# A macaron encoder block on one core: the opening pinned in written order with TensorE spreading the norm's gain row, and the mLSTM's score and state-read products issued in turn on two row halves

## The chip, the cores and the metric

One core of a Trainium2 chip runs the whole block in one launch. The metric is device microseconds from start to end of the program. The kernel before was run three times: 926.23, 925.30 and 924.71 us, median 925.3. One further execution was taken with the hardware profiler; all views and rows are of that one.

## The reference

Input x is 512 tokens of 1024 features, float32. The block adds three branches in turn:

```python
h = swiglu(rmsnorm(x, norm_ffn1_pre), w_ffn1_in, w_ffn1_out)
x = x + 0.5 * rmsnorm(h, norm_ffn1_post)
h = mixer(rmsnorm(x, norm_mix_pre), ...)
x = x + rmsnorm(h, norm_mix_post)
h = swiglu(rmsnorm(x, norm_ffn2_pre), w_ffn2_in, w_ffn2_out)
x = x + 0.5 * rmsnorm(h, norm_ffn2_post)
```

The feed-forward width is 2816. The mixer joins a gated convolution of three taps over 512 channels with an mLSTM of 4 heads (64 features of q and k, 128 of v) that runs forward and backward over the tokens. The mLSTM is computed in four chunks of 128 tokens. In each head and direction: scores `q kT` inside a chunk, weighted by a decay matrix and multiplied by v; a state `kT v` per chunk, carried from chunk to chunk; and the read of the state carried in, `q C`, added to the chunk's own part and divided by a denominator.

## The kernel before

**Layout and stages.** Tokens lie in four blocks of 128 (`tb`). A feed-forward net has its 2816 columns in 22 pairs of gate and up columns (`j`). Each pair of 128 columns is a product over 1024 features, on two row halves of 256 tokens (`th`). Weights stream from memory through SP's queue (`w_load`, L128 to L139), and every weight and activation is split into a high part (a cast on ACT, L273) and a low part (the difference, on VectorE or, for the first weights, on POOL: L274 and `ON_POOL`), so that a product is three: high by high, high by low, low by high. `w_get` takes a ready weight from a list and splits further ones ahead of need.

The first two pairs (`PLAIN`, four weights) are plain products, L421: for each of the four weights 24 products on tokens 0 to 255, then 24 each on tokens 256 to 511. From the third pair on, the products are those of a seven-product scheme (L400), for which `combine_x` (L325) forms sums of the normed x on VectorE.

**The opening.** SP issues x0 and x1 in halves, then the gain row of the first norm copied to all 128 partitions (L249, two halves of 256 KB), two weights, x2, x3, two weights, and then small vectors (L640 to L646), the gain `g_post1` and the gate weights `rawg`. TensorE meanwhile runs 24 products on zeros (L269). `pre_norm` (L348) squares a token block on ACT (L294), makes the scale on VectorE and POOL (L282, L284, L287), and multiplies x, scale and gain on VectorE (L353). `flip_q` (L314) turns the normed block feature-first: four transposes per half on TensorE into one bank (L318), a high cast on ACT, a low difference on VectorE, and a full copy on ACT (L323). Blocks 0 and 1 are turned ahead of the first product, blocks 2 and 3 between plain products, by hooks `(i, third)`: in the hook's place, ahead of a third of the i-th group of products.

**The mixer.** Columns of the convolution are products at L391 (`mm_cols`), interleaved by hand with the heads. `weigh_q` (L893) multiplies q by its decay: a tile per pair of heads holds, on rows 0 to 63 and 64 to 127, the two heads, and on its column halves the two directions (L902). `states` (L932) makes the states, two heads on two column halves of the array. `head_a(h)` makes the scores of one head, four chunks into one bank (L949), the decay's exponent (L954, then L956 on VectorE reading that bank), and their product (L966). `head_b(h)` makes P times V (L980, 8 products) and adds the state reads (L987, 6 products), then divides (L997 to L1008). `head_c` turns the head (L1021). `conv` has its taps at L838, L840 and L842.

Scores and reads contract over 64 features, so each uses half the rows of the array: `qk[es, ...]` with `es` the rows of the head.

**What sets the order.** The code is written out by hand, and the framework's scheduler orders the instructions on each engine by its own timeline; PSUM has eight banks in one pool, SBUF pools of a few buffers, and a new tile waits until the readers of the tile that last held its buffer are done.

## Time and profile before

| | |
|---|---|
| timed runs | 926.23, 925.30, 924.71 us; median 925.3 |
| profiled execution | 924.99 us, of it 923.3 in the span of its instructions |
| first product of the first pair (L421) | starts at 13.15 us |
| first product of the seven-product scheme (L400) | starts at 39.76 us |
| first scores (L949) to last reads (L987) | 442.5 to about 511.6 us |
| TensorE's waits for other engines, as the waits view lists them | 10.3 us in seven groups, 4.0 of them L318 for L353 |

A row of the timeline or the chain gives the start, the duration, the engine and the line, the tiles written and read, how many instructions are joined, and in brackets how long the engine was idle before and for whom it waited. A row of the groups gives, after the bar, busy time and mean duration in ns, and then idle time ahead of it. A row of the windows gives the busy time of TensorE (with how many instructions), of its weight loads, VectorE, ACT and POOL, and then the granted clock as a share of full speed, the DMA share and rate. Matmuls are pipelined: durations overlap, and the pace is read from the length of a chain piece divided by its count.

### The profile page before, as it was taken

How to read it: one execution, taken by the hardware profiler on the slowest of the kernel's cores; microseconds unless marked ns; L12 is line 12 of the kernel's file. 1: busy time of each engine (PE TensorE's matmuls, PEld its weight loads, DVE VectorE, ACT ScalarE, POOL GpSimd, SP SyncE). 2: the span in 40 equal slices, each digit the busy share in tenths (PEclk: the TensorE clock that was granted, in tenths of full speed). 3: DMA queues.
4: the chain of work that ended last, by engine and by line, in shares of the span. 5: the costliest groups of instructions: out<-in, count | busy, mean ns of one | idle time of the engine just before them, and what ended most of it. 6: DMA issues, size and time to landing. Idle time of an engine off the chain costs nothing.

```text
span 923.3 us, 15016 instructions
## 1 busy us (share of the span) xinstructions
PE 906.5 (98%) x6015; PEld 822.4 (89%) x6015; DVE 713.2 (77%) x1192; ACT 446.4 (48%) x753; POOL 42.3 (5%) x64
## 2 busy tenths in 40 slices
PE   7999999999999999999999999999999999999997
PEld 7999999999877888987888888999999999977885
DVE  5988988888988358496777736889888888999434
ACT  6645555555456226452424425645545544565311
POOL 3000000000012001000011000000000000000000
PEclk9999999999999999999999999999999999999999
DMA  8433434343344514231422501314343333343502
GB/s 246 146 92 92 138 105 125 92 117 95 100 136 139 180 46 115 61 100 46 117 90 69 160 23 30 104 51 137 92 129 101 109 104 97 106 149 100 172 4 88
DMA packets 126542, 96.99 MB, mean 105 GB/s; under 512 B 4212, under 2 KB 114824, under 8 KB 126472
## 3 DMA queue, kind: packets, MB, share of 16 engines
q1 hardware_dynamic: 126472, 96.03, 35.2%
q8 instruction: 47, 0.77, 0.3%
q14 instruction: 23, 0.19, 0.1%
HBM read 93.92 MB, written 2.10 MB: 104 GB/s over the span
## 4 chain that ended last, share of the span: by engine, by line
PE 89%; DVE 6%; ACT 1%; DMA 1%; issue 1%; SPq 0%; POOL 0%; DVEq 0%; POOLq 0%; ACTq 0%
PE ps L400 42%; PE ps L550 13%; PE ps L391 12%; PE ps L525 8%; PE ps L1063 5%; PE ps L421 4%; PE ps L913 2%; DVE big L274 2%; DVE wlo L274 2%; DVE big L492 1%; DMA raw<-in_w_ffn_in_dram 1%; PE ps L980 1%; PE ps L987 1%; PE ps L318 1%; ACT whi L273 0%
## 5 line engine op out<-in xcount | busy, mean ns | idle before, releaser
L274 DVE TENSOR_TENSOR wlo<-raw,whi 128x1024 fp32r<-128x1024 f32 x209 | 247.3, 1192 | 63.7 <-ACT whi L273 47.1
L273 ACT CAST whi<-raw 128x1024 fp32r<-128x1024 f32 x211 | 211.9, 1029 | 153.0 <-DVE raw L150 46.8
L400 PE MATMUL ps<-big,whi 128*128 128x256 f32 x1920 | 264.9, 280 | 0.0
L400 PEld LDWEIGHTS ps<-big,whi 128*128 128x128 f32 x1920 | 243.4, 188 | 0.9 <-ACT whi L273 0.2
L400 PE MATMUL ps<-big,wlo 128*128 128x256 f32 x960 | 150.9, 280 | 0.0
L400 PEld LDWEIGHTS ps<-big,wlo 128*128 128x128 f32 x960 | 129.2, 188 | 0.0
L550 PE MATMUL ps<-whi,big 128*128 128x512 f32 x384 | 122.3, 396 | 0.2 <-ACT whi L273 0.2
L550 PEld LDWEIGHTS ps<-whi,big 128*128 128x128 f32 x384 | 72.0, 188 | 17.7 <-ACT whi L273 0.7
L391 PE MATMUL ps<-big,whi 128*128 128x512 f32 (+1 forms) x384 | 79.8, 358 | 0.0
L525 PE MATMUL ps<-whi,big 128*128 128x512 f32 x240 | 76.1, 395 | 2.8 <-ACT big L273 2.6
L550 PE MATMUL ps<-wlo,big 128*128 128x512 f32 x192 | 75.6, 395 | 0.0
L391 PEld LDWEIGHTS ps<-big,whi 128*128 128x128 f32 x384 | 63.5, 188 | 10.8 <-issue 0.2
L400 PE MATMUL ps<-big,ws 128*128 128x256 f32 x480 | 65.3, 280 | 0.0
L400 PEld LDWEIGHTS ps<-big,ws 128*128 128x128 f32 x480 | 60.3, 188 | 0.0
L525 PEld LDWEIGHTS ps<-whi,big 128*128 128x128 f32 x240 | 44.7, 188 | 13.8 <-ACT big L273 3.5
L462 ACT COPY t<-ps 128x256 f32<-128x256 f32 x40 | 14.9, 372 | 71.4 <-PE ps L400 71.3
L273 ACT CAST big<-big 128x512 fp32r<-128x512 f32 (+2 forms) x68 | 36.1, 583 | 22.7 <-DVE big L492 11.2
L525 PE MATMUL ps<-wlo,big 128*128 128x512 f32 x120 | 44.8, 393 | 0.0
L550 PEld LDWEIGHTS ps<-wlo,big 128*128 128x128 f32 x192 | 36.1, 188 | 8.5
L391 PE MATMUL ps<-big,wlo 128*128 128x512 f32 (+1 forms) x192 | 41.1, 356 | 0.0
L274 DVE TENSOR_TENSOR big<-big,big 128x512 fp32r<-128x512 f32 (+2 forms) x68 | 40.7, 635 | 0.1
L391 PEld LDWEIGHTS ps<-big,wlo 128*128 128x128 f32 x192 | 32.1, 188 | 5.5
(207 smaller groups left out, 1149.6 us busy)
## 6 DMA issues: line engine op xcount, KB each, us to landing
raw<-in_w_ffn_in_dram SPq DMA_DIRECT2D x88, 512.0 KB, 4.8
raw<-in_w_ffn_out_dram SPq DMA_DIRECT2D x44, 512.0 KB, 4.3
raw<-in_w_mix_in_dram SPq DMA_DIRECT2D x24, 512.0 KB, 3.7
raw<-in_w_mix_out_dram SPq DMA_DIRECT2D x8, 512.0 KB, 3.4
raw<-in_w_ffn_out_dram SPq DMA_DIRECT2D x10, 256.0 KB, 4.2
out_dram<-x SPq DMA_DIRECT2D x8, 256.0 KB, 2.9
x<-in_x_dram SPq DMA_DIRECT2D x4, 256.0 KB, 4.5
x<-in_x_dram SPq DMA_DIRECT2D x2, 512.0 KB
```

The lines of the kernel that those rows point to most:

```text
L273: nc.scalar.copy(out=hi, in_=src)
L274: eng.tensor_tensor(out=lo, in0=src, in1=f32(hi), op=ALU.subtract)
L318: nc.tensor.transpose(out=pt[:, blk(k)], in_=xs[:, blk(4 * b + k)], identity=ident)
L391: nc.tensor.matmul(o, ww[:, k, :], xk(xT, xx, k, sl), start=n == 0, stop=n == 3 * KD - 1)
L400: nc.tensor.matmul(o, ww[:, k, :], x[xx][:, k, :], start=first and n == 0, stop=n == 11, skip_group_check=True)
L421: nc.tensor.matmul(o, ww[:, k, :], xq_hl(xq, (k // 4, th))[xx][:, k % 4, :], start=n == 0, stop=n == 3 * KD - 1)
L462: nc.scalar.copy(a_[:, h1], x[:, h0])
L492: nc.vector.tensor_tensor(out=o, in0=a_, in1=b_, op=op)
L525: nc.tensor.matmul(acc[tb + t][half], left[n][x][:, blk(t)], right[n][y], start=first and x == y == 0, stop=last_ and x == 1, skip_group_c ...
L550: nc.tensor.matmul(acc[tb][half], hT[hh][:, blk(tb)], w[ww][:, blk(half, 512)], start=fresh and hh == ww == 0, stop=k == NF - 1 and hh == ...
L913: nc.tensor.matmul(pv_, xk(xT, xx, k, blk(tb)), ww[:, k % 2, :], start=n == 0, stop=n == 3 * KD - 1)
L1063: nc.tensor.matmul(acc[half], yy[yi][:, k % 4, blk(tb)], wmo[k][wi][:, blk(half, 512)], start=(n == 0 and yi == 0 and wi == 0), stop=(n == ...
```

## The change

Two parts, which touch different stages.

**Opening.** All instructions ahead of the first seven-product are pinned in the order in which the code issues them. The gain row comes as one row of 4 KB, first on SP; TensorE spreads it by two float32 products of a column of ones with it, into two banks, after 12 of now 20 warm products, and VectorE reads the gain from PSUM. Blocks 0 and 1 are turned block by block instead of half by half, into four banks of their own, and their full copies move from ACT to VectorE. All four first weights have their low part on POOL. x2 and x3 are squared in one piece. The small vectors and two gains are issued later on SP, and the weights between x2 and x3.

**Mixer.** The q tile has directions on its row halves and heads on its column halves. Scores of both heads of a pair are issued in turn, chunk by chunk, each to its own bank, at the even head. The states are made per head with the two directions on the column halves. The state reads of both directions of one head are issued in turn on the two row halves.

```diff
-WARM = 24
+WARM = 20
-ON_POOL = (0, 1)
+ON_POOL = (0, 1, 2, 3)
...
+    g_row = gbp.tile([P, D], F32, tag="gb", name="g_row")
+    nc.sync.dma_start(g_row[0:1, :], a["norm_ffn1_pre"])
     x_load(0, 2)
     x_load(1, 2)
-    g_pre = gain("norm_ffn1_pre", 2)
     w_load(2)
     x_load(2)
+    w_load(1)
     x_load(3)
-    w_load(2)
+    w_load(1)
...
+    first = [ps() for _ in range(4)]
+    g_pre = [ps() for _ in range(2)]
+    for n in range(WARM):
+        pin(nc.tensor.matmul(pw[:, 0:256], warm[:, 0:P], warm, start=True, stop=True))
+        if n == 11:
+            for i in range(2):
+                pin(nc.tensor.matmul(g_pre[i], ones, g_row[0:1, blk(i, 512)], start=True, stop=True))
...
+    full = []
+    for tb in range(2):
+        for b in range(2):
+            full.append(flip_q(tb, xs[tb], xT1, (b,), first[2 * tb + b]))
+        if tb == 0:
+            for i in range(WARM2):
+                pin(nc.tensor.transpose(out=pw[:, 0:P], in_=xs[0][:, blk(i % 4)], identity=ident))
+        w_split(1)
+    for fn in full:
+        fn()
...
-                nc.vector.tensor_tensor(out=qt[:, blk(d, 512)], in0=pi, in1=qk[:, pr, 0:512], op=ALU.mult)
+                for e in range(2):
+                    es, ds = slice(e * DK, (e + 1) * DK), slice(d * DK, (d + 1) * DK)
+                    nc.vector.tensor_tensor(out=qt[ds, blk(e, 512)], in0=pi[es], in1=qk[es, pr, 0:512], op=ALU.mult)
...
-        pS = ps()
-        for c in range(NT):
-            nc.tensor.matmul(pS[:, blk(c)], qk[es, 2 + pr, blk(c)], qk[es, pr, blk(c)], start=True, stop=True)
+        if e == 0:
+            both = [ps(), ps()]
+            for c in range(NT):
+                for o in range(2):
+                    os_ = slice(o * DK, (o + 1) * DK)
+                    nc.tensor.matmul(both[o][:, blk(c)], qk[os_, 2 + pr, blk(c)], qk[os_, pr, blk(c)], start=True, stop=True)
+            scores[h], scores[h + 1] = both
+        pS = scores.pop(h)
...
-        for d in range(2):
-            for c in range(NT):
-                if before[d][c] >= 0:
-                    nc.tensor.matmul(
-                        dest[d][c], qt_pair[pr][es, d * 512 + c * P:d * 512 + (c + 1) * P],
-                        Cs[es, 2 * d + pr, before[d][c], :], start=False, stop=True, skip_group_check=True,
-                    )
+        for n in range(NT - 1):
+            for d in range(2):
+                c = [c for c in range(NT) if before[d][c] >= 0][n]
+                ds = slice(d * DK, (d + 1) * DK)
+                nc.tensor.matmul(
+                    dest[d][c], qt_pair[pr][ds, e * 512 + c * P:e * 512 + (c + 1) * P], Cs[ds, h, before[d][c], :],
+                    start=False, stop=True, skip_group_check=True,
+                )
```

In the changed kernel the lines have moved: L269 is L285, the spreading products are L288, L318 is L343, L353 is L383, L421 is L453, L400 is L431, L391 is L422, L949 is L1003, L956 is L1012, L987 is L1043, and L840 is L890. Three places on the engines:

TensorE at the start, from the last warm products to the first products; in the kernel before:

```order
L269 MATMUL ps_115<-warm 128x256
L318 MATMUL ps_167<-ident,t_7_141 128x128 x4
L610 MATMUL ps_115<-ident,t_7_141 128x128 x4
L318 MATMUL ps_181<-ident,t_13_154 128x128 x4
L318 MATMUL ps_189<-ident,t_7_141 128x128 x4
L318 MATMUL ps_199<-ident,t_13_154 128x128 x4
L421 MATMUL ps_247<-big_172,whi_235 128x256 x4
```

and in the changed one, from the twelfth warm product (eight warm products stand behind the two that spread the gain, of which the last is shown; `t_12` is the normed block 0, `t_18` block 1):

```order
L285 MATMUL ps_116<-warm 128x256
L288 MATMUL ps_121<-g_row,ones 128x512
L288 MATMUL ps_122<-g_row,ones 128x512
...
L285 MATMUL ps_116<-warm 128x256
L343 MATMUL ps_117<-ident,t_12_146 128x128 x4
L343 MATMUL ps_118<-ident,t_12_146 128x128 x4
L650 MATMUL ps_116<-ident,t_12_146 128x128 x4
L343 MATMUL ps_119<-ident,t_18_159 128x128 x4
L343 MATMUL ps_120<-ident,t_18_159 128x128 x4
L453 MATMUL ps_235<-big_176,whi_192 128x256 x4
```

Both halves of block 0 are now turned ahead of block 1, and the gain's two products stand inside the warm ones. The second place is TensorE from the scores of head 1 to the reads of head 0, which follow them (`t_663` and, after, `t_661` is head 0's weighted score tile); before:

```order
L949 MATMUL ps_4871<-big_4301 128x128 x4
L954 MATMUL ps_4877<-big_4311 128x512
L954 MATMUL ps_4886<-big_4311 128x512
L980 MATMUL ps_4896<-big_4318,t_663_4730 128x129 x2
L980 MATMUL ps_4897<-big_4318,t_663_4730 128x129 x2
L980 MATMUL ps_4902<-big_4318,t_663_4730 128x129 x2
L980 MATMUL ps_4903<-big_4318,t_663_4730 128x129 x2
L987 MATMUL ps_4896<-big_4573,qt_4629 128x129
L987 MATMUL ps_4897<-big_4573,qt_4629 128x129 x2
L987 MATMUL ps_4902<-big_4573,qt_4629 128x129 x2
L987 MATMUL ps_4903<-big_4573,qt_4629 128x129
```

and after, where the scores of head 1 were made with those of head 0, so that only head 1's exponent and head 0's P times V and reads stand here:

```order
L1010 MATMUL ps_4874<-big_4304 128x512
L1010 MATMUL ps_4883<-big_4304 128x512
L1035 MATMUL ps_4893<-big_4311,t_661_4732 128x129 x2
L1035 MATMUL ps_4894<-big_4311,t_661_4732 128x129 x2
L1035 MATMUL ps_4899<-big_4311,t_661_4732 128x129 x2
L1035 MATMUL ps_4900<-big_4311,t_661_4732 128x129 x2
L1043 MATMUL ps_4893<-big_4566,qt_4622 128x129
L1043 MATMUL ps_4899<-big_4566,qt_4622 128x129
L1043 MATMUL ps_4894<-big_4566,qt_4622 128x129
L1043 MATMUL ps_4899<-big_4566,qt_4622 128x129
L1043 MATMUL ps_4894<-big_4566,qt_4622 128x129
L1043 MATMUL ps_4900<-big_4566,qt_4622 128x129
```

The reads now go back and forth between the banks of the two directions, and so between the row halves. The third place is VectorE at head 2's exponent; before:

```order
L836 TENSOR_TENSOR t_705_4977<-ps_4979,t_705_4977 128x512
L274 TENSOR_TENSOR wlo_5290<-raw_5287,whi_5289 128x1024
L838 TENSOR_SCALAR t_710_5011<-t_705_4977,vec 128x512
L956 TENSOR_SCALAR t_712_5020<-ps_5021,big_4573 128x128 x4
L956 TENSOR_SCALAR t_712_5020<-ps_5030,big_4573 128x128 x4
L840 SCALAR_TENSOR_TENSOR t_710_5011<-t_705_4977,vec,t_710_5011 128x511
```

and after (`ps_5032` is the bank of the second direction's exponent):

```order
L886 TENSOR_TENSOR t_702_4974<-ps_4976,t_702_4974 128x512
L294 TENSOR_TENSOR wlo_5287<-raw_5284,whi_5286 128x1024
L888 TENSOR_SCALAR t_707_5008<-t_702_4974,vec 128x512
L1012 TENSOR_SCALAR t_710_5022<-ps_5023,big_4566 128x128 x4
L1012 TENSOR_SCALAR t_710_5022<-ps_5032,big_4566 128x128 x2
L890 SCALAR_TENSOR_TENSOR t_707_5008<-t_702_4974,vec,t_707_5008 128x511
L1012 TENSOR_SCALAR t_710_5022<-ps_5032,big_4566 128x128 x2
```

One tap of the convolution has moved ahead of the last two reads of that bank.

## The prediction

> **What bounds the kernel now.** I read the page first: its busy row and its chain.

> ```profile
> PE 906.5 (98%) x6015; PEld 822.4 (89%) x6015; DVE 713.2 (77%) x1192; ACT 446.4 (48%) x753; POOL 42.3 (5%) x64
> PE 89%; DVE 6%; ACT 1%; DMA 1%; issue 1%; SPq 0%; POOL 0%; DVEq 0%; POOLq 0%; ACTq 0%
> ```

> TensorE is busy for 906.5 of 923.3 us and is 89% of the chain. A change can pay in two ways: by shortening what TensorE does, or by closing one of its few gaps. The waits of TensorE name the largest gap:

> ```profile
> PE ps L318 <- DVE t L353: 4.0, 2, 3.2
> ```

> Two waits of the first transposes for the normed x on VectorE, 4.0 us together, are in the opening. The timeline (start, duration, engine) shows where:

> ```profile
> 0.80 1.80 SPq L243 DMA_DIRECT2D x<-in_x_dram  x4
> 1.34 5.30 PE L269 MATMUL ps<-warm 128*128 128x256 bf16 x24 [1.34 <-POOL gbias L644]
> 5.34 0.55 POOL L287 TENSOR_TENSOR rs<-rs,nhalf 128x1 f32<-128x1 f32 x1 [3.68 <-DVE rs L284]
> 7.82 0.56 POOL L287 TENSOR_TENSOR rs<-rs,nhalf 128x1 f32<-128x1 f32 x1 [1.93 <-DVE rs L284]
> 9.02 2.74 DVE L353 SCALAR_TENSOR_TENSOR t<-x,rs,gb 128x512 f32<-128x512 f32 x4 [1.35 <-DMA gb<-in_norm_ffn_pre_dram]
> 9.83 0.66 PE L318 MATMUL ps<-ident,t 128*128 128x128 f32 x4 [3.18 <-DVE t L353]
> 10.52 0.59 ACT L273 CAST big<-ps 128x512 fp32r<-128x512 f32 x1 [3.04 <-PE ps L318]
> 10.76 2.74 PE L318 MATMUL ps<-ident,t 128*128 128x128 f32 x12
> 11.21 1.05 ACT L273 CAST whi<-raw 128x1024 fp32r<-128x1024 f32 x1
> 12.34 2.38 POOL L274 TENSOR_TENSOR wlo<-raw,whi 128x1024 fp32r<-128x1024 f32 x1 [3.96 <-ACT whi L273]
> 13.15 2.80 PE L421 MATMUL ps<-big,whi 128*128 128x256 f32 x16
> 15.78 1.10 PE L421 MATMUL ps<-big,wlo 128*128 128x256 f32 x8
> 16.72 2.04 PE L421 MATMUL ps<-big,whi 128*128 128x256 f32 x16
> 24.52 1.29 PE L318 MATMUL ps<-ident,t 128*128 128x128 f32 x8 [0.79 <-DVE t L353]
> 39.76 1.11 PE L400 MATMUL ps<-big,whi 128*128 128x256 f32 x8
> ```

> The reader is to see three things. VectorE had the scale of x0 at 5.89 (5.34+0.55) and that of x1 at 8.38 (7.82+0.56), and started at 9.02 because the norm's broadcast row was still in its DMA. TensorE stood still from 6.64 to 9.83. And the twelve transposes at 10.76 took 0.23 us each, the first four 0.17. The windows of one microsecond (busy by engine, then PEclk) say why:

> ```profile
> 10.00:11.00 1.00, 1.00 (x10) 1.00 (x10) 1.00 (x2) 0.48 (x1) 0.00 (x0) 0.88 1.23 320
> 11.00:12.00 1.00, 1.00 (x6) 1.00 (x5) 1.00 (x3) 0.89 (x2) 0.00 (x0) 0.50 0.98 366
> 13.00:14.00 1.00, 1.00 (x7) 1.00 (x5) 0.72 (x2) 1.00 (x3) 1.00 (x1) 0.50 0.97 366
> 14.00:15.00 1.00, 1.00 (x8) 0.79 (x8) 1.00 (x2) 1.00 (x2) 0.72 (x1) 0.91 1.12 348
> ```

> From about 10.9 to 14.3 us the granted clock was 0.50: half speed, a little over a microsecond after the pause. The second place is the mixer, from its chain (start, length):

> ```profile
> 442.60 1.08 PE ps L949 x8
> 444.35 2.79 PE ps L932 x48
> 460.19 1.79 PE ps L980 x16
> 461.97 1.53 PE ps L987 x12
> ```

> These are one head's scores, all states, one head's P times V and its state reads. Each product of the code is two passes in the trace (four products of a head are x8). A pass on the whole array costs 1.79/16 = 0.112 us. The scores, on half the rows, cost 1.08/8 = 0.135 with the change of tile, and the reads 1.53/12 = 0.128: half the rows are no cheaper. The states, whose products alternate between two column halves, cost 2.79/48 = 0.058: two at a time. Mixer and opening are apart, so I cost them apart.

> **The opening, part by part.** The norm's row comes as 4 KB at the head of SP's queue instead of 2 x 256 KB behind x. An issue on SP takes 1.80/4 = 0.45, so x lands some 0.4 later, and the scales of x0 and x1 are ready at 5.34+0.55+0.4 = 6.3 and 8.38+0.4 = 8.8. TensorE spreads the row after 12 warm products: 5.30/24 = 0.22 us each, so from 4.0. Two fp32 products of 512 columns, two passes each: by 0.112 per 128 columns a pass is 0.45, four are 1.8 at full clock, 3.6 at half: g stands in PSUM at 5.8 to 7.6. No row shows a product of one row; less than the streaming I exclude, as L949 and L987 show that few rows save nothing. Eight warm products follow (0.9 to 1.8), so TensorE reaches the transposes at about 8 to 9.4.

> VectorE norms x0 from 6.3 to 7.6 and x1 from 8.8 (four products in 2.74, 0.69 each). A PSUM operand costs it nothing, by these two rows of the same size, one reading PSUM, one not:

> ```profile
> L274 DVE TENSOR_TENSOR big<-ps,big 128x512 fp32r<-128x512 f32 x8 | 5.2, 684 | 0.7 <-ACT big L273 0.7
> L150 DVE TENSOR_TENSOR t<-raw 128x512 f32<-128x512 f32 x1 | 0.7, 693 | 0.9 <-DMA raw<-in_w_ffn_in_dram 0.9
> ```

> So the wait for g goes, and next late is x1's scale: x1 is normed at 8.8 to 10.2, its transposes (0.66 each at full clock) end near 10.9. ACT has four casts of 0.59 and one of the weight (1.05) before the last x half; the first weight's high part is ready at about 11.3 against 12.26, and its low part on POOL, 2.38 later, at 13.7. The first group of 24 products starts at about 11.8 and its last eight wait for the low part: end 13.7+0.94 = 14.6, between 14.0 (POOL early) and 15.0. Before, group two starts at 16.72. From there TensorE alone counts, if nothing waits: three groups, two sets of transposes of 1.29, and the 96 products of the second row half. The chain prices a product:

> ```profile
> 25.81 14.11 PE ps L421 x120
> 39.92 192.35 PE ps L400 x1632
> ```

> 14.11/120 = 0.1176, so 72+96 = 168 products are 19.76 and, with the transposes, 22.3: L400 (there L431) would start at 36.3 to 37.3, not 39.76. That is 2.5 to 3.5, and includes the second wait of 0.79. **I take 2.8.**

> What hides the rest. POOL makes four low parts instead of two: 4 x 2.39 from 11.3 is 20.9 with nothing between. They are wanted at the last third of each group: the second at 14.6+1.88 = 16.5 (ready 16.1), the third at 19.3 (18.5), the fourth, behind a transpose set, at 23.4 (20.9); the smallest margin is 0.4. VectorE loses these two (1.22 each) and takes four copies of 128x512 from ACT. No row shows that copy; 0.68 (L274 above) bounds it above, since it reads one operand fewer, ACT's 0.6 below: 2.4 to 2.7 against 2.44, nothing. Its cover thereafter is thin:

> ```profile
> 35.00:40.00 5.00, 5.00 (x45) 5.00 (x45) 5.00 (x6) 5.00 (x6) 0.00 (x0) 1.00 0.20 57
> ```

> VectorE is busy throughout here, combining x for L431. If it moves by less than TensorE, what TensorE gains beyond is waited for; x2's norms start one group earlier in the new order, so VectorE's work comes forward too, by 2.1 to 2.7 as I count. So the opening's lower end is 1.3, its upper 3.5. The moved small loads and gains (SP) land tens of microseconds ahead of their use in either order, and the first products wait for x and weights issued earlier: nothing.

> The clock can move this. The half-clock stretch follows the long pause by about a microsecond. With the pause cut to about one microsecond at most it should not come. If it came at 10.9 to 14.3 as before, the first group would take some 1 us more and the gain be 1.8; if it fell wholly on products (14.3 to 17.7), 1.7 of product time more, and the gain 1.3. [...]

> **The mixer, part by part.** Scores: two heads' 16 passes alternate on rows 0-63 and 64-127 and in two banks. If they pair as the column halves do, 16 x 0.058 and one entry of about 0.16 are 1.09, what one head cost: two pairs save 2 x 1.09 = 2.2. Reads: 12 passes at 0.058 and the entry are 0.86 against 1.53: 4 x 0.67 = 2.7. Weights could be the limit, as each half brings its own:

> ```profile
> L932 PEld LDWEIGHTS ps<-big,big 128*64 128x64 f32 x48 | 2.6, 136 | 0.4 <-issue 0.4
> L949 PEld LDWEIGHTS ps<-big 64*128 64x128 f32 x32 | 3.9, 187 | 1.4 <-issue 1.4
> ```

> On column halves 48 loads of 136 ns fit in 2.6 us, over two at a time; so loads to separate tiles do overlap. For row halves no row shows it; ends: nothing saved, and 4.9. I take the full pairing, as the nearest row. [...]

> New cost. In head 2's iteration the convolution's next product takes the bank that the last L956 (now L1012) reads, and VectorE now places L890 (before L840) ahead of the last two of eight.

> ```profile
> 477.10 2.15 DVE L956 TENSOR_SCALAR t<-ps,big 128x128 f32<-128x128 f32 x8
> 479.17 1.03 DVE L840 SCALAR_TENSOR_TENSOR t<-t,vec,t 128x511 f32<-128x511 f32 x1
> 480.99 0.73 DVE L842 SCALAR_TENSOR_TENSOR t<-t,vec,t 128x511 f32<-128x511 f32 x1
> 480.21 3.95 PE L391 MATMUL ps<-big,whi 128*128 128x512 f32 x16
> ```

> TensorE gets there at 480.21-0.67 = 479.54; VectorE, which ended at 479.25, has one operation of 511 columns put in (0.73 at L842, up to 1.03 at L840) and ends at 480.0 to 480.3. A wait of 0.4 to 0.75; I take 0.45. The weighing of q becomes eight operations of 64x512 for four of 128x512. Their time goes by columns, 2.7 us more, if 64 rows cost as 128:

> ```profile
> 428.83 2.47 DVE L902 TENSOR_TENSOR qt<-ps,big 128x512 f32<-128x512 f32 x4
> 439.31 1.23 DVE L274 TENSOR_TENSOR wlo<-raw,whi 128x1024 fp32r<-128x1024 f32 x1 [7.61 <-ACT whi L273]
> ```

> VectorE idles 7.61 us right behind, and q is read first at 461.97: hidden. States alternate halves as before: nothing. **The mixer: 2.2+2.7-0.45 = 4.4 less.**

> **The sum.** The profiled execution took 924.99 (span 923.3 and 1.7 around it), 0.3 under the median of 925.3. 924.99-2.8-4.4 = 917.8; with the 0.3, **918.1**.

> **The rivals.**
> (a) Row halves do not pair: nothing shows them to. The mixer then gains nothing, the conv wait goes with it (TensorE comes 0.67 later), and 925.3-2.8 = 922.5. Chance 0.15.
> (b) The opening keeps a half-clock stretch, or VectorE follows late: gain 1.3 there, 925.3-1.3-4.4 = 919.6. For it: VectorE at 5.00 of 5.00. Against: no pause as long. Chance 0.2.
> (c) Slower: a change of row half costs as a change of tile does. The entries are dearer than a pass: (1.08-8x0.112) = 0.18. There are 7 changes in each of two score sequences and 5 in each of four read sequences, 34. At 0.18 each with no pairing that is 6.1, less 2.8: 928.6. It makes the kernel slower from 2.8/34 = 0.08 per change. Against: the states change half at each product and pay nothing. [...] Chance 0.05.
> (d) The two parts of the opening and the mixer do what they say but a new wait, on a PSUM bank or VectorE, returns most of it: 924 to 925. Chance 0.08.
> The forecast has 0.52. A measurement of this kernel can tell 0.2%, 1.85 us, from no change: under 923.45 is faster. Forecast, (a) and (b) nearly all lie there: 0.86; (d) and a poor (a) give 0.09 within; (c) 0.05 slower. The range takes the unknown costs downward (3.5 and 4.9 of gain: 916.9, and half a microsecond of bounds) and upward holds (a) with a smaller opening: 916.2 to 923.3.

> **What would show it.** Right: no wait of L343 on L383 over 1 us; no 0.50 in PEclk past 9 us; L431 starting at 36.3 to 37.5; L1003 as x16 in about 1.1 us and L1043 x12 in 0.86; one wait of about half a microsecond ahead of the convolution in head 2's iteration. Wrong: L1003 x16 in 2.2 us (a), over 2.5 (c); a PEclk of 0.50 among L453 or waits of L431 on VectorE (b).

## The result and the profile after

The changed kernel took 914.89, 915.36, 917.67 and 917.74 us, median 916.51, against 925.0 for the kernel before beside it: ratio 0.9904, 95% interval 0.9885 to 0.9923. That is 8.5 us less by the medians and 8.9 by the ratio, where 7.2 were forecast. Five more executions, taken later beside an experiment, had 915.99, 917.13, 917.69, 917.82 and 918.09: ratio 0.9914 (0.9900 to 0.9927). Over all nine the median is 917.67. They do not scatter evenly: most lie near 917.7, some near 915.3. Much of what follows is about these two values. The profiled execution (915.36, span 913.7) is of the lower kind.

The busy row and the chain of the page:

```profile
PE 900.1 (99%) x6015; PEld 816.7 (89%) x6015; DVE 716.2 (78%) x1196; ACT 444.6 (49%) x745; POOL 44.7 (5%) x67
PE 93%; DVE 4%; ACT 1%; issue 1%; DMA 1%; SPq 0%; POOL 0%; DVEq 0%; POOLq 0%; ACTq 0%
```

TensorE's busy time fell by 6.4 us, its idle time by 3.2. Its waits, as far as they touch the change:

```profile
PE ps L343 <- DVE t L383: 1.1, 1, 1.1
PE ps L422 <- DVE den L1053: 0.2, 1, 0.2
```

The 4.0 us of the first transposes have become 1.1, and there is one new small wait, at the convolution. The timeline of the opening:

```profile
1.33 2.74 PE L285 MATMUL ps<-warm 128*128 128x256 bf16 x12 [1.33 <-POOL warm L278]
4.00 2.22 PE L288 MATMUL ps<-g_row,ones 1*128 1x512 f32 x4
6.16 1.05 PE L285 MATMUL ps<-warm 128*128 128x256 bf16 x8
6.31 1.41 DVE L383 SCALAR_TENSOR_TENSOR t<-x,rs,ps 128x512 f32<-128x512 f32 x2 [0.74 <-POOL rs L310]
9.95 1.31 PE L343 MATMUL ps<-ident,t 128*128 128x128 f32 x8 [1.09 <-DVE t L383]
11.28 2.46 PE L453 MATMUL ps<-big,whi 128*128 128x256 f32 x16
36.24 1.11 PE L431 MATMUL ps<-big,whi 128*128 128x256 f32 x8
```

The gain stands in PSUM at 6.2, block 0's norm starts at 6.31 behind its own scale, and what is left is the wait for block 1. The first products start at 11.28 instead of 13.15 and the first seven-product at 36.24 instead of 39.76: 3.5 us. The pace tells the clock here, since PEclk prints 1.00 ahead of its first record: the twelve warm products ran at 0.21 us each, the eight behind the spread at half of that. The mixer, from the chain:

```profile
438.51 1.09 PE ps L1003 x16
440.26 3.07 PE ps L983 x48
454.62 0.46 PE ps L1010 x2
455.08 1.78 PE ps L1035 x16
456.87 0.87 PE ps L1043 x12
```

Two heads' scores take what one took (1.09), and twelve reads 0.87 for 1.53: 0.068 and 0.073 us a pass, where the states' passes on two column halves took 0.058 before (2.79 for 48). The row halves pair here as the column halves did. Placed side by side product by product, the lead over the kernel before is 3.52 us at the first seven-product, 4.09 at the first scores, 8.62 at the last reads and 9.53 at the last product.

### The profile page after: what moved, and what is told of

Its sections match the earlier page's. It is cut to its first block, busy times and chain, and to the rows that moved or that the text cites. A ratio compares the mean times of both kernels' runs of the same rounds, so it can differ in the third digit from the quotient of the medians.

```text
span 913.7 us, 15022 instructions
## 1 busy us (share of the span) xinstructions
PE 900.1 (99%) x6015; PEld 816.7 (89%) x6015; DVE 716.2 (78%) x1196; ACT 444.6 (49%) x745; POOL 44.7 (5%) x67
## 4 chain that ended last, share of the span: by engine, by line
PE 93%; DVE 4%; ACT 1%; issue 1%; DMA 1%; SPq 0%; POOL 0%; DVEq 0%; POOLq 0%; ACTq 0%
PE ps L431 43%; PE ps L589 13%; PE ps L422 12%; PE ps L564 9%; PE ps L453 5%; PE ps L1119 5%; PE ps L965 2%; DVE big L294 1%; DVE wlo L294 1%; PE ps L343 1%; DVE big L531 1%; PE ps L1035 1%; DMA x<-in_x_dram 1%; PE ps L983 0%; PE ps L391 0%
## 5 line engine op out<-in xcount | busy, mean ns | idle before, releaser
L431 PE MATMUL ps<-big,whi 128*128 128x256 f32 x1920 | 264.8, 280 | 0.0
L431 PEld LDWEIGHTS ps<-big,whi 128*128 128x128 f32 x1920 | 243.5, 188 | 0.5
L431 PE MATMUL ps<-big,wlo 128*128 128x256 f32 x960 | 150.9, 280 | 0.0
L431 PEld LDWEIGHTS ps<-big,wlo 128*128 128x128 f32 x960 | 129.3, 188 | 0.0
L422 PE MATMUL ps<-big,whi 128*128 128x512 f32 (+1 forms) x384 | 79.8, 358 | 0.2 <-DVE den L1053 0.2
L422 PEld LDWEIGHTS ps<-big,whi 128*128 128x128 f32 x384 | 63.5, 188 | 11.2 <-PE ps L1077 0.4
L431 PE MATMUL ps<-big,ws 128*128 128x256 f32 x480 | 65.3, 280 | 0.0
L431 PEld LDWEIGHTS ps<-big,ws 128*128 128x128 f32 x480 | 60.3, 188 | 0.0
L422 PE MATMUL ps<-big,wlo 128*128 128x512 f32 (+1 forms) x192 | 41.1, 356 | 0.0
L422 PEld LDWEIGHTS ps<-big,wlo 128*128 128x128 f32 x192 | 32.1, 188 | 5.5
```

Of the source, the lines that this page charges most:

```text
L422: nc.tensor.matmul(o, ww[:, k, :], xk(xT, xx, k, sl), start=n == 0, stop=n == 3 * KD - 1)
L431: pin(nc.tensor.matmul(o, ww[:, k, :], x[xx][:, k, :], start=first and n == 0, stop=n == 11, skip_group_check=True))
```

## The experiments

**The parts alone.** First the changed opening with the mixer of before, and the reverse; in each, `weigh_q`, `states`, `head_a`, `head_b` and the tiles `pm` and `par` are the other kernel's (the scores as an example, in the direction of the first):

```diff
-        if e == 0:
-            both = [ps(), ps()]
...
+        pS = ps()
+        for c in range(NT):
+            nc.tensor.matmul(pS[:, blk(c)], qk[es, 2 + pr, blk(c)], qk[es, pr, blk(c)], start=True, stop=True)
...
```

> The opening of the changed kernel with the mixer of the kernel before. Theory (opening and mixer are apart and add up): the first seven-product starts 3.5 us earlier than before, the start of the scores 4.1 earlier, the time falls by 3.5 to 4.4 us. Rival (part of the opening's lead is waited for later, as VectorE is full there, and the rest of the 8.9 is the mixer's): the lead at the first scores is under 3 and the time falls by 2 to 3 us.

> The mixer of the changed kernel with the opening of the kernel before. Theory: one pair's scores x16 in 1.1 us, reads x12 in 0.87, one wait of 0.4 at the convolution in head 2's iteration, the time falls by 4.3 to 4.7 us. Rival (the parts do not add up): the fall is under 3.5 or over 5.5.

The opening alone: 922.4 (919.89, then 922.14 to 923.08), ratio 0.9964 (0.9951 to 0.9976), 3.1 us under the 925.5 of the kernel before beside it. The mixer alone: 920.29, ratio 0.9943 (0.9930 to 0.9955), 5.2 under it and so above the 4.3 to 4.7 expected. In the trace the mixer alone gains 4.52 between the first scores and the last reads, the changed kernel 4.53, and 3.1 and 5.2 are 8.3 of the 8.5: the parts are apart and add, as the theory had it. The opening alone leads by only 1.9 at the first seven-product, less than either the 3.5 of the changed kernel or the theory's range, and 1.8 of that is left at the scores: it is kept, not waited for later. So the rival's lead (under 3 at the scores) came and its reason did not: the same opening gave 3.5 in one execution and 1.9 in another. What each part of the opening is worth (the gain row, the turning block by block, the low parts on POOL, the written order) was not tried one by one. The mixer kernel, whose opening is that of before, shows where to look. Its windows and its wait:

```profile
8.00:9.00 1.00, 0.00 (x0) 0.00 (x0) 0.16 (x1) 0.17 (x2) 0.49 (x1) 0.59 1.07 306
14.00:15.00 1.00, 1.00 (x6) 1.00 (x5) 0.71 (x2) 0.86 (x2) 1.00 (x1) 0.50 1.12 351
15.00:16.00 1.00, 1.00 (x8) 0.85 (x8) 0.88 (x2) 1.00 (x2) 0.17 (x1) 1.00 1.15 346
PE ps L318 <- DVE t L353: 5.0, 2, 4.2
```

Here the clock was at half from 8.2 to 15.0, twice as long as in the profile of before, and its opening ended 1.0 us later than that of before, with nothing changed in it.

**Order or layout.** The same tiles, banks and row halves, but one half's products after the other's:

```diff
-            for c in range(NT):
-                for o in range(2):
+            for o in range(2):
+                for c in range(NT):
...
-        for n in range(NT - 1):
-            for d in range(2):
+        for d in range(2):
+            for n in range(NT - 1):
```

> The changed kernel with its q tile, its banks and its row halves, but scores and reads issued one row half after the other instead of in turn. Theory (the gain is that products of two row halves run at the same time when they are neighbours in the queue): x16 scores take about 2.0 us and x12 reads about 1.5, as before, and the kernel loses 4 to 5 us against the changed one. Rival (the gain is from two banks or the layout, not from the order): x16 stay at 1.1 and the time stays within 1 us of the changed one.

```profile
438.64 1.64 PE ps L1003 x16
457.55 1.19 PE ps L1043 x12
```

Neither came. Median 919.5 (917.46 to 920.33), ratio 0.9933 (0.9921 to 0.9946), 1.8 us over the median of the changed kernel's nine executions; the lead gained in the mixer is 2.6 instead of 4.5. Sixteen passes one by one would be about 2.0 us (an estimate: 16 at 0.112 and an entry of about 0.16), all paired 1.09; they took 1.64. The single records of the scores show it; which half a record belongs to is read from its place in two rows of starts 0.11 apart. In TensorE's program the four products of one half stand ahead of the four of the other. Five passes of the first half start (438.57 to 439.12), then the first pass of the other half starts 5 ns after the fifth, while three of the first half are still to come; after that they run in pairs until the first half is done. By this reading TensorE started, in this run, a product of the other half ahead of an older one, the fourth of the first half, past three waiting passes. So the gain is in passes of the two halves that run at the same time, and of the orders tried only issuing in turn got all of it (1.09 us for 1.64). Whether it also needs a bank for each half was not tried.

**The new wait.** The taps of the convolution on VectorE, put behind the eight exponent operations of head 2:

```diff
         if h + 1 < NH:
             head_a(h + 1)
+        if h == 1:
+            with tc.issue_after(latest["E"].ins):
+                cs["taps"]()
         head_b(h)
```

> The changed kernel with the convolution's taps on VectorE behind all eight exponent operations of head 2, so that the bank comes free earlier. Theory: the wait ahead of the convolution in that iteration (0.2 for VectorE and as much in the queue) goes, the time falls by 0.3 to 0.45 us, less than these rounds can tell. Rival (another reader of a bank ends just as late): the convolution's product starts no earlier.

The place in the changed kernel, on VectorE and TensorE:

```profile
471.26 1.64 DVE L1012 TENSOR_SCALAR t<-ps,big 128x128 f32<-128x128 f32 x6
472.81 0.74 DVE L890 SCALAR_TENSOR_TENSOR t<-t,vec,t 128x511 f32<-128x511 f32 x1
473.47 0.60 DVE L1012 TENSOR_SCALAR t<-ps,big 128x128 f32<-128x128 f32 x2
474.22 3.94 PE L422 MATMUL ps<-big,whi 128*128 128x512 f32 x16 [0.19 <-DVE den L1053]
```

and with the taps moved:

```profile
470.73 2.15 DVE L1017 TENSOR_SCALAR t<-ps,big 128x128 f32<-128x128 f32 x8
472.80 1.03 DVE L891 SCALAR_TENSOR_TENSOR t<-t,vec,t 128x511 f32<-128x511 f32 x1
473.25 3.02 PE L422 MATMUL ps<-big,whi 128*128 128x512 f32 x12
```

From the transposes ahead of it (L1077 at 473.37, here 472.84) the product now starts 0.41 later instead of 0.85: 0.44 us back, as the forecast's 0.45 said. The median, 917.41, shows nothing of it, as expected; its executions are 914.44 and 917.18 to 917.84.

**The clock.** The remaining runs ask what parts the two values. First the kernel before with warm products until shortly before its transposes:

```diff
-WARM = 24
+WARM = 46
```

> The kernel before with 46 warm products instead of 24, so that TensorE has no pause until the transposes. Theory (the half clock of before's opening comes from the pause): PEclk shows no 0.50 after the warm products, the first group starts about 1 us earlier, the time falls by 1 to 2 us. Rival (the half clock comes at a fixed time whatever TensorE does): a stretch of 0.50 still lies among the first products and the time stays within 0.5 us of before.

```profile
13.89 5.13 PE L421 MATMUL ps<-big,whi 128*128 128x256 f32 x28 [1.71 <-ACT big L273]
13.00:14.00 1.00, 0.11 (x1) 0.12 (x2) 0.18 (x2) 1.00 (x3) 1.00 (x1) 1.00 1.05 381
14.00:15.00 1.00, 1.00 (x6) 1.00 (x7) 0.72 (x2) 1.00 (x3) 1.00 (x2) 0.64 1.11 341
17.00:18.00 1.00, 1.00 (x8) 1.00 (x7) 0.16 (x1) 1.00 (x4) 0.23 (x1) 0.66 0.21 54
```

Ratio 0.9999 (0.9991 to 1.0008): no gain, so the expected size failed, and both signs of the rival came, half clock among the first products and an unchanged time. But not at a fixed time: the clock stayed full until 14.28 (0.64 is 72% of that microsecond at half), and then was at half until 17.68, where in the profile of before it was at half from 10.77 to 14.18. The scheduler had put both weight casts ahead of the second cast of x on ACT, TensorE paused 1.7 us for that cast, and half clock came behind that pause. So half clock came behind a pause here too, at another place (an earlier pause, from 7.8 to 9.5, it did not follow), and was 3.4 us long, as in the profile of before (3.41); in the mixer kernel it was twice that (6.8). In the profiles the changes fall at other times each: half clock began at 14.28 here, at 10.77 and 8.2 there.

A pause can not be the whole of it, since the changed kernel has little pause ahead of its spread. Here is its opening in an execution of the higher kind (917.69):

```profile
4.01 3.78 PE L288 MATMUL ps<-g_row,ones 1*128 1x512 f32 x4
7.72 1.89 PE L285 MATMUL ps<-warm 128*128 128x256 bf16 x8
9.39 1.92 PE L343 MATMUL ps<-ident,t 128*128 128x128 f32 x8
13.69 2.23 PE L453 MATMUL ps<-big,whi 128*128 128x256 f32 x16
```

Everything to the first transposes ran at half: the spread in 3.78 instead of 2.22, the warm products behind it in 1.89 instead of 1.05, and the products start 2.4 us later, although TensorE was busy from 1.33 on. That suggested that products of one row do not raise the clock. Two kernels with eight later warm products replaced test it, by one-row products and by products on all rows of the same length:

```diff
-    for n in range(WARM):
+    for n in range(12):
...
+    for i in range(2):
+        pin(nc.tensor.matmul(pw, ones, g_row[0:1, blk(i, 512)], start=True, stop=True))
```

and

```diff
+    for i in range(8):
+        pin(nc.tensor.matmul(pw[:, 0:P], ident, ident, start=True, stop=True))
```

> The changed kernel with the eight later warm products replaced by a second pair of one-row products of the same kind into a spare bank (their result is not used). Theory (the clock's monitor counts a product of one row as little or nothing): in nearly every execution the clock is at half through the first products, or falls to half before them, and the time is 1.5 to 3 us above the changed kernel's lowest. Rival (any product counts as busy): TensorE is busy without a pause from 1.3 us, so the clock is full from 4.8 at the latest and stays full, and the time is within 1 us of the changed kernel's lowest.

> The changed kernel with the eight later warm products replaced by eight float32 products on all 128 rows of 128 columns each, as long together as the second pair of one-row products in the run beside it. Theory (only rows in use count): the clock is full from 8 us at the latest and stays so; executions are 1 us or more faster in the median than those with a second one-row pair. Rival (the kind of product does not matter): both runs have the same median within 0.5 us.

With one-row products:

```profile
4.01 3.78 PE L287 MATMUL ps<-g_row,ones 1*128 1x512 f32 x4
7.58 3.62 PE L289 MATMUL ps<-g_row,ones 1*128 1x512 f32 x4
11.13 1.97 PE L344 MATMUL ps<-ident,t 128*128 128x128 f32 x8
13.74 1.14 PE L344 MATMUL ps<-ident,t 128*128 128x128 f32 x8
```

and with products on all rows:

```profile
6.15 2.05 PE L289 MATMUL ps<-ident 128*128 128x128 f32 x16
```

In the first, TensorE was busy without a pause from 1.34 to 11.1 us, and still at half clock at 11.13 (eight transposes in 1.97); it was full about 13.9, behind 2.8 us of transposes. A clock that rises with any busy time does not fit that. Medians 920.07 (917.12 to 920.98) and 917.60, 2.5 us apart; but the second run's executions fall into two groups of three, 915.25 to 916.13 and 919.05 to 919.36, and its median lies between them. That its profile is of the lower group is chance; the upper has none, and whether its clock was full by 8 us, as expected, is not known. The trace of the first run is the stronger evidence.

Other traces say the same. In the blocked run of above the clock rose at 3.99 and fell again at 7.40, though TensorE was idle for only 0.44 us between (in the profile after, the clock stayed full behind a pause of 1.09):

```profile
4.00 1.98 PE L288 MATMUL ps<-g_row,ones 1*128 1x512 f32 x4
5.92 1.05 PE L285 MATMUL ps<-warm 128*128 128x256 bf16 x8
7.43 1.97 PE L343 MATMUL ps<-ident,t 128*128 128x128 f32 x8 [0.47 <-DVE t L383]
8.00:9.00 1.00, 1.00 (x7) 1.00 (x6) 0.26 (x3) 0.55 (x3) 0.49 (x1) 0.50 1.18 360
```

Nearly two thirds of its work there was the one-row spread. And changes of the clock lie 3.41 us or twice that apart: 3.41 from 10.77 to 14.18 in the profile of before, 3.41 from 3.99 to 7.40 in the blocked run, 6.8 from 8.2 to 15.0 in the mixer kernel. Counted back from the first rise in such steps, which is an estimate, as no record lies ahead of it, five stretches that TensorE filled with work stayed at half: one in the opening alone, two with the second one-row pair, two in the execution of 917.69. In these, at most 2.0 us were work on all rows; the stretch ahead of the rise in the blocked run had 2.66 us of such work. The expectations below call such a step a window; what sets it no run shows.

Then a spread on all rows. These kernels, here and below, also have the taps moved. The first attempt cleared 127 rows under the gain's:

```diff
-    nc.sync.dma_start(g_row[0:1, :], a["norm_ffn1_pre"])
+    nc.vector.memset(g_row, 0.0)
     x_load(0, 2)
+    nc.sync.dma_start(g_row[0:1, :], a["norm_ffn1_pre"])
...
-                pin(nc.tensor.matmul(g_pre[i], ones, g_row[0:1, blk(i, 512)], start=True, stop=True))
+                pin(nc.tensor.matmul(g_pre[i], ones, g_row[:, blk(i, 512)], start=True, stop=True))
```

> The changed kernel with the gain spread by products over 128 rows (127 of them zero, cleared on VectorE first, so the gain's row is issued behind part of x), and with the convolution's taps behind the exponents. Theory: the spread counts as work for the clock, so the slow half of the changed kernel's executions goes; the median falls to 914 to 915.5 us. Rival (the spread among two values has another cause): the executions still fall into two groups 2.5 us apart, median near 917.

```profile
5.02 3.75 PE L289 MATMUL ps<-g_row,ones 128*128 128x512 f32 x4 [0.94 <-DMA g_row<-in_norm_ffn_pre_dram]
8.57 1.62 PE L286 MATMUL ps<-warm 128*128 128x256 bf16 x8
```

A miss: 917.85 (917.12 to 918.94). The row landed at 5.0, TensorE paused 0.94 us for it, the clock rose at 9.75 only, and the spread ran at half. Its five executions are one group instead of two, but at the wrong end. The second attempt brings the row as 8 by 128, which needs a clearing of 0.17 us only, and picks the rows out:

```diff
+    g8 = const.tile([P, P], F32, name="g8")
+    nc.vector.memset(g8, 0.0)
+    pick = gbp.tile([P, D], F32, tag="gb", name="pick")
     x_load(0, 2)
+    nc.sync.dma_start(g8[0:8, :], a["norm_ffn1_pre"][0].rearrange("(c p) -> c p", p=P))
...
+    nc.vector.tensor_copy(ch(pick), ident[:, 0:8].broadcast_to([P, 8, P]))
...
-        if n == 11:
-            for i in range(2):
-                pin(nc.tensor.matmul(g_pre[i], ones, g_row[0:1, blk(i, 512)], start=True, stop=True))
+        if n == 13:
+            for i in range(8):
+                pin(nc.tensor.matmul(g_pre[i // 4][:, blk(i % 4)], pick[:, blk(i)], g8, start=True, stop=True))
```

> The changed kernel with the gain loaded as 8 rows of 128 and spread by eight products on all 128 rows (a tile of selectors made on VectorE from the identity; the rows below the eighth are zero), as long together as the one-row products, after 14 of the 20 warm products, and with the convolution's taps behind the exponents. Theory (rows in use are what the clock's monitor counts, and the changed kernel's executions fall into two groups by whether the clock rises ahead of the spread): TensorE works on all rows from 1.3 us without a pause, the clock is full from 7.5 at the latest; the group near 917.6 goes, the median is 914.5 to 916. Rival (the groups have another cause, or zeros do not count as work): median 917 to 918, one execution in four near 915.

> The changed kernel itself once more, on the chip of the run beside it. Theory: executions near 915.1 and near 917.6, about one in four of the first kind (the clock's window must end between 4.0 and 4.8 us, 0.8 of 3.41); the profile is of the first kind if and only if PEclk rises between 4.0 and 4.8. Rival (the two groups belong to chips): all executions in one group.

915.13 (914.32, 914.76, 915.51, 916.88), as expected, beside 917.69 for the changed kernel on the same chip; against before 0.9893 (0.9880 to 0.9907). The moved taps are 0.4 of this. The changed kernel's five were the two values again, so they do not belong to chips; one of five, 915.99, is near the lower. The profiled execution of the new one was its slowest and shows why:

```profile
4.44 2.28 PE L289 MATMUL ps<-g,pick 128*128 128x128 f32 x16
6.55 0.82 PE L286 MATMUL ps<-warm 128*128 128x256 bf16 x6
10.31 1.31 PE L344 MATMUL ps<-ident,t 128*128 128x128 f32 x8 [1.62 <-DVE t L384]
11.64 3.66 PE L454 MATMUL ps<-big,whi 128*128 128x256 f32 x16
12.00:13.00 1.00, 1.00 (x7) 1.00 (x7) 1.00 (x3) 1.00 (x2) 0.94 (x1) 0.50 1.12 337
```

The spread ran at full clock, but the pause ahead of block 1's transposes was 1.6 us, and half clock, which by the expectation should have been gone, fell on the first products (11.80 to 15.22). The last pair of runs fills that pause, and repeats the kernel:

```diff
-WARM2 = 4
+WARM2 = 12
```

> The kernel with selectors and taps moved, and 12 instead of 4 filling transposes between the turns of block 0 and block 1, so that the pause of 1.1 to 1.6 us there shrinks. Theory: the clock cannot fall to half at a window's end near 11.8, the slowest of the executions (916.9) go, the median is 914 to 915. Rival (the filling delays block 1's transposes by as much as it saves): median 915 to 916, as the run beside it.

> The kernel with selectors and taps moved, again, on the chip of the run beside it. Theory: median 914.5 to 916 as before, most executions under 915.6, few near 917. Rival (the first result was a lucky draw of clock phases): two groups with most near 917.5.

The repetition: 915.94 (914.09, 915.86, 916.01, 916.22); the median came as expected, but one of four lies under 915.6, where most were to. Its profile, again the slowest, shows the same pause (1.84 us) and the same half clock (10.99 to 14.40). The eight executions of this kernel have a median of 915.7, 2 us under the nine of the changed one. All eight lie under 917, six of the nine over it, so it looks the better version; the intervals of the two ratios overlap. The filled one: 914.33, 915.5, 916.79, 917.86, median 916.14, above theory and rival. Its profile (914.33) has no half clock in the opening once it has risen, but two executions are no better than the changed kernel's; filling is not shown to help, and what happened in those two is open, as they have no profile.

## Why the prediction came out as it did, point by point

**The wait for the gain** went as forecast; the gain stood in PSUM at 6.2 in one profile and 7.8 in another (5.8 to 7.6 forecast), and the wait left over is block 1's, 1.1 us (up to 1 forecast). POOL's four low parts were never waited for, and VectorE, thin as its cover was, did not take the lead back: 3.5 us at the first seven-product and still at 71 us.

**The clock** is the step that failed. The forecast had it that with the pause cut "it should not come", and counted one number, 2.8, for the opening. It had given the opening a range of 1.3 to 3.5, with half clock in it only as a stretch behind a pause. What came is not one number: leads at the first seven-product of 3.5 (changed kernel), 1.9 (opening alone), 1.3 (changed again) and 4.0 (with the taps moved), for the same instructions. By the clock records of the seven profiles with the one-row spread, the clock rose between 4.0 and 4.8 us in four (three of them the lowest executions of their kernels, one the second lowest) and between 10.6 and 14.0 in three (none of them the lowest). The twelve warm products, 1.33 to 4.0, fill 2.7 of a stretch's 3.41 us, and the one-row spread behind them left the clock at half when it went on to 11.1; so, by an estimate, an early rise needs a stretch that ends between 4.0 and 4.8, 0.8 of 3.41 or 23%. Of the 14 executions of the changed kernel and of that with the taps moved, 4 (29%) lie under 916. I had asked whether the spread would be slow at half clock, not whether it keeps the clock at half. Rival (b) had the right size for the lowest lead, 1.3, but not the reason: neither VectorE nor a stretch behind the pause, but half clock from the start, through the whole spread (4.01 to 7.72) and the warm products behind it. Where the clock rose early, the forecast of 2.8 was too small mainly by its transposes: the second group of products starts at 14.52 (14.6 forecast), but the two sets of transposes hold the products up by 0.8 each, for the 1.29 that I had taken.

Two readings were off by little. The rows of before give half clock from 10.77 to 14.18, not 10.9 to 14.3. And if half clock falls wholly on products, 2.8 less 1.7 is 1.1, not 1.3, so the lower end was too high and (b) is 919.8.

**The mixer** came as worked out, 4.53 for 4.4. Term by term: scores 2.16 for 2.2; reads 4 x 0.66 = 2.6 for 2.7; the convolution's wait 0.44 for 0.45. Two small terms were missing and nearly cancel: the exponents' two products take 0.46 instead of 0.67 where no scores stand ahead of them, twice 0.2 gained, and the states take 3.07 instead of 2.79, 0.28 lost, where I had put nothing. Why the states are slower was not tried. The weighing of q cost 5.5 us on VectorE for 2.5, 3.0 more for the 2.7 counted, and nothing waited, as forecast:

```profile
L954 DVE TENSOR_TENSOR qt<-ps,big 64x512 f32<-64x512 f32 x8 | 5.5, 687 | 0.1
```

**Rivals (a) and (c)** fell: sixteen passes in 1.09 us leave no price for a change of row half. I had taken full pairing from the nearest row, the column halves; it held. **(d)**, a new wait that returns most of it, did not come: the one new wait is 0.44.

**The sum** was 7.2. In the profiled execution the lead is 9.5: 0.7 more from the opening, 0.1 from the mixer, and 1.5 outside both, 0.6 up to the scores and 0.9 behind the mixer. The first 0.6 came between 72 and 100 us, where the mixer kernel, with the opening of before, gained the same and the opening alone nothing: it goes with the execution, not with the change. The 0.9 is there with the opening alone too (0.9) and hardly with the mixer alone (0.16); what it is stays open. Over nine executions the median is 7.3 under 925.0, nearly the forecast; that is luck: as far as the profiles tell, two errors of opposite sign, an opening worth less than 2.8 in most executions, and gains outside both parts that had no term.

## What to carry to other kernels

The gain at the start of this kernel was worth what the clock made of it: the same instructions led by 1.3 to 4.0 us. With the spread on all rows instead of one, from 4.44 us on, the median was 915.7 for 917.67, of which the moved taps are 0.4; where that spread had waited 0.94 us for its row it was 917.85, and filling the pause behind the spread showed nothing more (916.14 for 915.94). So try early products on all rows ahead of the first real ones, and judge the opening by several executions, not by one trace. Products on half of the rows were worth pairing: with the two halves next to each other in the queue sixteen passes took 1.09 us, one half after the other 1.64 (here each half wrote a bank of its own; one bank was not tried). And where a change frees TensorE time ahead of a bank's reuse, look on VectorE for what stands ahead of the bank's last reader: moving the convolution's taps brought 0.44 us of trace here.
